# A hybrid convolution and recurrence block on one core: a first stage with joint adaLN scale and shift, and the output gate's steps placed later

## The chip, the cores and the metric

The kernel runs on one core of a Trainium2 chip. The time is the device time of one execution in microseconds (us); where a kernel was run several times, the median counts. A profiled execution gives a trace of every instruction. TensorE is the matrix engine (PE in the rows, PEld is its loading of weights), VectorE is DVE, ScalarE is ACT, GpSimd is POOL, SyncE is SP. ACTq and SPq are DMA issues of these engines.

## The reference, cut to what matters

One layer over 256 latent tokens `x` and 256 context tokens `ctx`, 2048 channels, all float32.

```python
sh, sc, gt = split(silu(c) @ w_ada + b_ada, 3)        # adaLN of the latents; sh_c, sc_c from c_ctx
hn     = rmsnorm(x, norm_g)   * (1 + sc)   + sh
hn_ctx = rmsnorm(ctx, norm_g) * (1 + sc_c) + sh_c
a, g, z_c, xr, z_r, gc, gr = split(hn @ w_in + b_in)  # 2048 columns each
...                                                    # y_conv = conformer(a, g, z_c) @ w_conv_out
...                                                    # y_rnn  = rglru(xr, both directions, state from ctx) * silu(z_r) @ w_rnn_out
y = sigmoid(gc) * y_conv + sigmoid(gr) * y_rnn
x = x + gt * (y @ w_o)
return rmsnorm(x, final_g)
```

For the context only the columns `xr` of `w_in` are needed.

## The kernel before

Channels lie on the 128 partitions in 16 tiles, tokens (256 context, 256 latent) along the free axis. Each float32 operand is split in two parts, `hi` and `lo`, and a product is made of three: hi·hi, hi·lo and lo·hi. For weights ScalarE makes `hi` (`wsplit_hi`, L184) and VectorE `lo` (`wsplit_lo`, L189). For some of them (`adding`, every fourth half from stage AD0 to AD1) `lo` comes instead from ScalarE's negated copy (L195) and a transfer on GpSimd's queue that adds the weight again from DRAM (`wsplit_add`, L196). The order of all work is written out by hand; every engine runs its instructions in the order in which the program emits them, and a transfer waits on the engine that issues it until its buffer is free.

**First stage** (L248 to L370). The input comes in five pieces (L257); the first holds the channel tiles 7 to 4, and the sum of squares `ms` starts with tile 7. VectorE and ScalarE make the squares, TensorE sums them (`stat_mm`, L239), then `1/rms` is made and broadcast (`rms_back`, L290). In parallel the adaLN columns come as 64 pieces `adaraw` of 512 KB, for each group of one or two channel tiles first those of the scale (`part` 1), then those of the shift (`part` 0); TensorE multiplies them by `csil` (`ada_mms`, L220) into one PSUM tile, ScalarE copies it to `row` (L344), and `ada_fin` sums four partial rows with a selector (L227), adds the bias (L229) and forms `(1 + sc) * norm_g` (L232). VectorE scales a tile by `rinv` (L294), applies scale and shift (L300), and `split` gives `xh`, `xl`. The products of a group (`products`, L245: eight output blocks, six of them kept in PSUM banks, two through a spare bank `part` and added by VectorE at L319 and L321) run as a list `todo` while the next group is prepared; TA to TD say how many of them go between which steps.

**Dense part.** 152 stages `s`: the input projection for the recurrence and its gates, for the convolution (`a`, `g`, `z_c`), then five projections with the tokens as output rows in four chunks of 512 columns, four slots of two halves each: `gr`, `rnn`, `gc`, `conv`, `o`. Stage 88 to 103 are `rnn`.

**The output gate.** `gt` for the latents is needed as a row over all partitions, in four chunks of 512 columns. VectorE accumulates it in 64 steps, 16 for a chunk (`gt_step`, L904: `gt_chunk += csil * gt_raw`); a load of 512 KB serves two steps, and two buffers (GTB) hold such loads; the next load is issued when the second step of a pair is emitted. Four calls (GTD) after the last step of a chunk a product with ones (L917) sums the partitions, and ScalarE copies the result back (L918). Steps are called from the slots of the projections: up to GTG in each slot of `gc` (once the side work has started the gate), GTN in each slot of `conv`, GTO in each half slot of `o`. At the chunk's evacuation the rest is forced:

```python
def evac_o(c, i, acc):
    while c not in gt_done:
        gt_steps(1)
```

The last chunk of `o` has two slots of the usual form; its last two slots are written half by half (`for i in range(2)`: 24 products for token half `i`, then `evac_o(3, i, ...)`, then `finish(i)`), without calls of steps besides those of `evac_o`.

Of the kernel before, what the change touches and what calls it, by code (L numbers as in the profile page):

```python
# [8 lines left out]
F32 = mybir.dt.float32  # L9
# [3 lines left out]
PSUM = bass.MemoryType.PSUM  # L13
ADD, MUL, SUB = ALU.add, ALU.mult, ALU.subtract
# [14 lines left out]
GTB, GTG, GTN, GTO, GTD = 2, 2, 2, 1, 4  # L29
TA, TB, TC, TD = 1, 2, 1, 1  # L30
AD0, AD1, ADN = 24, 104, 4
# [53 lines left out]
def block_kernel(ctx, tc, xcat, xtok, fgrow, brow, par, wada, wgt, bgt, wearly, wall, wgate, out):  # L85
# [19 lines left out]
    def pall(name):  # L105
        a, w = _PCOLS[name]
        return pt[:, a:a + w]
# [12 lines left out]
    sh2 = const.tile([P, KT, 2], F32, name="sh2")  # L120
    sc2 = const.tile([P, KT, 2], F32, name="sc2")
# [101 lines left out]
    def ada_fin(row, part, k0, n):  # L223

        tp = ps0.tile([P, 2, 2], F32, tag="ada", name="tp")[:, :n]
        for i in range(n):
            PE.matmul(out=tp[:, i, :], lhsT=row[:, P * i:P * i + P], rhs=pall("sel"), start=True, stop=True)  # L227
        dst = (sh2, sc2)[part][:, k0:k0 + n, :]
        V.tensor_tensor(out=dst, in0=tp, in1=pc("b_ada", 32 * part + 2 * k0, 2 * n).rearrange("p (k v) -> p k v", v=2),  # L229
                        op=ADD)  # L230
        if part == 1:
            V.scalar_tensor_tensor(out=dst, in0=dst, scalar=1.0,  # L232
                                   in1=pc("norm_g", 2 * k0, 2 * n).rearrange("p (k v) -> p k v", v=2),
                                   op0=ADD, op1=MUL)
# [13 lines left out]
    with ExitStack() as st:  # L248
        ps0 = st.enter_context(tc.tile_pool(name="ps0", bufs=1, space=PSUM))
        sp = st.enter_context(tc.tile_pool(name="start", bufs=1))  # L250
        ada_p = st.enter_context(tc.tile_pool(name="ada", bufs=8))
# [4 lines left out]
        for a, b in ((0, 4), (4, 8), (8, 12), (12, 14), (14, 16)):  # L256
            SP.dma_start(out=xlo[:, a:b] if b <= 8 else xhi[:, a - 8:b - 8], in_=xcat[:, a:b, :])  # L257
# [6 lines left out]
        t4 = sp.tile([P, 4], F32, name="t4")  # L264
        A.activation(out=r4[:, 0:1], in_=epst, func=AF.Sqrt)
        ms = psum("ms")
        for n, k in enumerate([*range(7, -1, -1), *range(8, KT)]):
            sq = row_p.tile([P, 512], F32, tag="sq", name="sq", bufs=4)
# [4 lines left out]
            stat_mm(ms, sq, n)  # L273
        sqs = sp.tile([P, 512], F32, name="sqs")
        V.tensor_copy(sqs, ms)
# [5 lines left out]
        rsqrt(r4, t4, s4)  # L281
        dgs = []
        for t in range(4):
            dgs.append(row_p.tile([P, P], F32, tag="dg", name="dg", bufs=4))
            V.tensor_scalar(out=dgs[t], in0=pall("ident"), scalar1=r4[:, t:t + 1], scalar2=None, op0=MUL)

        def rms_back():
            tot = psum("tot")
            for t in range(4):
                PE.matmul(out=tot[:, P * t:P * t + P], lhsT=unit, rhs=dgs[t], start=True, stop=True)  # L290
            return tot

        def scale(k):
            V.tensor_tensor(out=xin(k), in0=xin(k), in1=rinv, op=MUL)  # L294

        def normalise(ks):
            for s in range(2):
                for k in ks:
                    xk = xin(k)[:, T * s:T * s + T]
                    V.tensor_scalar(out=xk, in0=xk, scalar1=sc2[:, k, 1 - s:2 - s], scalar2=sh2[:, k, 1 - s:2 - s],  # L300
                                    op0=MUL, op1=ADD)
            for k in ks:
                split(xh[:, k], xl[:, k], xin(k).rearrange("p (s t) -> p s t", s=2))

        def products(m, ks, ws):
            tr3 = []
            for k, (hi, lo) in zip(ks, ws):
                c = P * m
                tr3 += [(hi[:, c:c + P], xh[:, k]), (hi[:, c:c + P], xl[:, k]), (lo[:, c:c + P], xh[:, k])]
            if m < NPS:  # L310
                mm3(acc0[m].rearrange("p (s t) -> p s t", s=2), ks[0] == 0, ks[-1] == KT - 1, tr3)
# [20 lines left out]
        nraw = 0  # L332
        for j, (k0, n) in enumerate(groups()):
            ks = range(k0, k0 + n)
            ws = []
            for part in (1, 0):
                acc = ps0.tile([P, T], F32, tag="ada", name="ada")[:, :P * n]
                for rnd in range(2 * n):
                    raw = ada_p.tile([P, 1024], F32, tag="ada", name="adaraw")
                    SP.dma_start(out=raw, in_=wada[nraw])  # L340
                    nraw += 1
                    ada_mms(acc, raw, rnd, n)
                row = row_p.tile([P, T], F32, tag="row", name="row", bufs=2)[:, :P * n]
                A.activation(out=row, in_=acc, func=AF.Copy)  # L344
                if part == 1:
                    wr = [load(wearly[k], P * NEARLY) for k in ks]
                    if k0 == 8:
                        parameters()
                run_todo(TA if part else TB)
                if part == 1 and j == 0:  # L350
                    tot = rms_back()
                ada_fin(row, part, k0, n)
                if part == 1 and j == 0:
                    V.tensor_copy(rinv, tot)
                    acc0 = {m: psum(f"xr{m}") for m in range(NPS)}
                    scale(0)
                run_todo(TC if part else TD)
                if part == 1:
                    for k in ks:
                        if k:  # L360
                            scale(k)
                    ws = [wsplit(w, P * NEARLY) for w in wr]
            normalise(ks)
            run_todo(NEARLY)
            if k0 > 8 and prepare:
                prepare.pop(0)()
            todo.extend([lambda m=m, ks=ks, ws=ws: products(m, ks, ws) for m in FIRST])
# [681 lines left out]
    def finish(i):  # L1049
# [118 lines left out]
```

## Time and profile before

| | |
|---|---|
| median of 3 runs | 1126.0 us (1125.2 to 1127.42) |
| profiled execution, its own time | 1123.41 us |
| span of its trace | 1121.6 us |
| TensorE busy | 1094.8 us, 98% |
| VectorE busy | 900.6 us, 80% |
| ScalarE busy | 657.5 us, 59% |
| bytes read | 253.31 MB |

The span is from the first instruction to the last; the own time is 1.8 us more. Rows give a start and a duration in us from the start of the span; durations of matrix records overlap, so a busy TensorE says that it had work, not how dense it was. Behind a row, in brackets, stands how long its engine was idle before it and what ended that. The granted clock column (PEclk) is a share of full speed.

### The profile page before, as it was taken

What the parts mean: (1) busy time and instruction counts of PE and PEld (TensorE: products, weight loads), DVE (VectorE), ACT (ScalarE), POOL (GpSimd) and SP (SyncE); (2) the same over time, 40 slices, a digit from 0 to 9 for tenths busy, and PEclk for the clock granted to TensorE, in tenths of its full rate; (3) what the DMA queues carried; (4) which work ended last, traced back from release to release, by engine and by line L of the source; (5) the groups of instructions that cost most, each with busy time, mean ns of one, the idle gap of its engine ahead of it and who ended that gap; (6) DMA issues with size and microseconds to landing.
All of it is one profiled execution on the core that took longest, in us unless ns stands there. A gap on an engine that the chain in (4) does not pass through costs nothing.

```text
span 1121.6 us, 15861 instructions
## 1 busy us (share of the span) xinstructions
PE 1094.8 (98%) x5788; PEld 876.6 (78%) x5788; DVE 900.6 (80%) x1541; ACT 657.5 (59%) x894; POOL 34.9 (3%) x44
## 2 busy tenths in 40 slices
PE   5999999999999999999999999999999999999996
PEld 3777777777788888788888887888877877788885
DVE  5554587887799787888999899899976967888885
ACT  4222269867788889776565645554536934445443
POOL 0000000000000000000000000000000000000000
PEclk9999999999999999999999999999999999999999
DMA  9998533433355877878888888888874678988872
GB/s 376 398 409 326 220 119 125 132 115 122 106 160 168 209 224 191 230 197 243 238 227 250 219 245 252 227 250 246 238 224 150 191 243 298 322 307 300 287 266 94
DMA packets 74528, 256.45 MB, mean 229 GB/s; under 512 B 8273, under 2 KB 12497, under 8 KB 74065
## 3 DMA queue, kind: packets, MB, share of 16 engines
q1 hardware_dynamic: 68114, 233.42, 61.5%
q0 software_dynamic: 5760, 20.97, 10.4%
q10 hardware_dynamic: 576, 1.05, 0.2%
q8 instruction: 45, 0.74, 0.2%
q14 instruction: 33, 0.27, 0.1%
HBM read 253.31 MB, written 2.10 MB: 228 GB/s over the span
## 4 chain that ended last, share of the span: by engine, by line
PE 79%; DMA 10%; DVE 5%; ACT 2%; issue 2%; SPq 0%; ACTq 0%; DVEq 0%; POOLq 0%
PE acc L602 20%; PE y L613 16%; PE acc L605 10%; PE acc L245 8%; PE o L613 8%; PE xr L245 6%; DMA wlo<-in_wall_dram 5%; PE gate L491 5%; DMA raw<-in_wall_dram 4%; PE ada L220 2%; PE part L245 2%; DVE wlo L189 2%; DVE zc L904 1%; ACT whi L184 1%; PE ms L239 1%
## 5 line engine op out<-in xcount | busy, mean ns | idle before, releaser
L184 ACT ACTIVATE whi<-raw 128x1024 fp32r<-128x1024 f32 x304 | 321.2, 1058 | 300.8 <-PE y L613 79.8
L189 DVE TENSOR_TENSOR wlo<-raw,whi 128x1024 fp32r<-128x1024 f32 x264 | 320.7, 1218 | 64.9 <-ACT whi L184 61.1
L602 PE MATMUL acc<-xx,whi 128*128 128x512 f32 x1024 | 265.0, 401 | 0.0
L613 PE MATMUL y<-whi,xx 128*128 128x512 f32 x1024 | 256.0, 392 | 0.8 <-ACT whi L184 0.8
L613 PEld LDWEIGHTS y<-whi,xx 128*128 128x128 f32 x1024 | 190.8, 188 | 43.5 <-issue 2.5
L602 PEld LDWEIGHTS acc<-xx,whi 128*128 128x128 f32 x1024 | 185.7, 189 | 43.6 <-issue 9.6
L722 DVE SCALAR_TENSOR_TENSOR cv<-hbuf,pt,cv 128x196 f32<-128x196 f32 (+14 forms) x480 | 184.1, 445 | 10.1 <-ACT cv L713 9.7
L605 PEld LDWEIGHTS acc<-xx,wlo 128*128 128x128 f32 x1024 | 139.5, 190 | 11.1 <-DMA wlo<-in_wall_dram 1.1
L605 PE MATMUL acc<-xx,wlo 128*128 128x256 f32 x1024 | 143.0, 282 | 0.3 <-DMA wlo<-in_wall_dram 0.3
L613 PE MATMUL y<-wlo,xx 128*128 128x512 f32 x512 | 137.9, 391 | 3.3 <-DMA wlo<-in_wall_dram 2.7
L613 PEld LDWEIGHTS y<-wlo,xx 128*128 128x128 f32 x512 | 95.5, 188 | 25.8 <-DMA wlo<-in_wall_dram 5.0
L480 DVE SCALAR_TENSOR_TENSOR xc<-xr,pt,xc 128x510 f32<-128x510 f32 (+2 forms) x96 | 70.7, 740 | 0.2
L613 PE MATMUL o<-whi,xx 128*128 128x512 f32 x256 | 65.3, 395 | 0.0
L245 PE MATMUL acc<-xx,whi 128*128 128x512 f32 x256 | 65.2, 407 | 0.0
L245 PE MATMUL xr<-xx,whi 128*128 128x512 f32 x192 | 62.6, 406 | 0.6 <-ACT xx L174 0.4
L491 PE MATMUL gate<-xc,gw 128*128 128x512 f32 x128 | 60.0, 592 | 0.0
L196 POOL DMA_DIRECT2D wlo<-in_wall_dram x40 | 34.6, 866 | 788.8 <-ACT wlo L195 419.2
L245 PEld LDWEIGHTS acc<-xx,whi 128*128 128x128 f32 x256 | 47.8, 188 | 14.2 <-issue 4.8
L613 PEld LDWEIGHTS o<-whi,xx 128*128 128x128 f32 x256 | 47.7, 188 | 10.6 <-issue 0.7
L904 DVE SCALAR_TENSOR_TENSOR zc<-gtraw,csil,zc 128x512 f32<-128x512 f32 x64 | 47.8, 747 | 5.4 <-DMA gtraw<-in_wgt_dram 4.7
L195 ACT ACTIVATE wlo<-raw 128x1024 fp32r<-128x1024 f32 x40 | 41.9, 1049 | 2.5 <-PE y L613 2.0
L344 ACT ACTIVATE row<-ada 128x128 f32<-128x128 f32 (+1 forms) x22 | 7.1, 325 | 60.0 <-PE ada L220 60.0
(178 smaller groups left out, 1048.4 us busy)
## 6 DMA issues: line engine op xcount, KB each, us to landing
raw<-in_wall_dram SPq DMA_DIRECT2D x304, 512.0 KB, 4.5
adaraw<-in_wada_dram SPq DMA_DIRECT2D x64, 512.0 KB, 8.3
wlo<-in_wall_dram POOLq DMA_DIRECT2D x40, 512.0 KB, 7.9
gtraw<-in_wgt_dram SPq DMA_DIRECT2D x32, 512.0 KB, 4.6
raw<-in_wearly_dram SPq DMA_DIRECT2D x16, 512.0 KB, 9.4
gw<-in_wgate_dram SPq DMA_DIRECT2D x32, 128.0 KB, 3.5
hbuf<-in_xcat_dram SPq DMA_DIRECT2D x2, 1024.0 KB, 6.3
gbias<-in_brow_dram SPq DMA_DIRECT2D x8, 256.0 KB, 6.4
```

What stands on the lines that cost most here:

```text
L184: A.activation(out=hi, in_=raw, func=AF.Copy)
L189: V.tensor_tensor(out=lo, in0=raw, in1=hi.bitcast(F32), op=SUB)
L195: A.activation(out=lo, in_=raw, func=AF.Copy, scale=-1.0)
L196: nc.gpsimd.dma_start(out=lo, in_=src, accum_op=ADD)
L245: PE.matmul(out=acc, lhsT=w, rhs=x, start=(first and i == 0), stop=(last and i == n - 1))
L480: V.scalar_tensor_tensor(out=o, in0=i, scalar=w, in1=o, op0=MUL, op1=ADD)
L491: PE.matmul(out=acc, lhsT=u["gw"][:, c:c + 128], rhs=u["xc"], start=True, stop=True)
L602: PE.matmul(out=acc, lhsT=hi[:, 128 * kk:128 * kk + 128], rhs=xx[:, k, 1], start=(k == 0), stop=False)
L605: PE.matmul(out=acc[:, 0], lhsT=lo[:, 128 * kk:128 * kk + 128], rhs=xh[:, k, 1], start=False, stop=(k == KT - 1))
L613: PE.matmul(out=acc, lhsT=y[:, k, seg, P * i:P * i + P], rhs=w[:, 512 * kk:512 * kk + 512], start=(leading and k == 0 and y is xh), stop=( ...
L722: V.scalar_tensor_tensor(out=o, in0=i, scalar=hdw[:, m * CW + j:m * CW + j + 1], in1=o, op0=MUL, op1=ADD)
L904: V.scalar_tensor_tensor(out=gt_chunk(c), in0=gt_raw[0][:, 512 * (k % 2):512 * (k % 2) + 512], scalar=csil[:, k, 0:1], in1=gt_chunk(c), op ...
```

## The change

- Scale and shift of a group are made together: both accumulators in one PSUM tile, one copy to `row`, `PE.transpose` of its tiles and one `tensor_reduce` on VectorE in place of the selector products; the adaLN pieces of both parts come ahead of the group's early weights, ten buffers hold them instead of eight.
- The multiplication by `1/rms` is fused with the scale; the shift is added in the two split operations. `1/rms` is broadcast by a product with a stride-0 operand instead of diagonal tiles.
- The first input piece is issued by ScalarE, the others by SyncE. One adaLN round stands ahead of the end of the sum of squares. The squares take the weights' buffers.
- The list of products is placed anew: TS products ahead of a group's adaLN sums, TA and TB after them, the rest at the end; the first group's list is ordered hi parts first.
- GTN goes from 2 to 1, AD1 from 104 to 98 (37 adding transfers, not 40).
- In `finish` the last of the four output pieces goes from ScalarE to VectorE and SyncE's queue.

```diff
-GTB, GTG, GTN, GTO, GTD = 2, 2, 2, 1, 4
-TA, TB, TC, TD = 1, 2, 1, 1
-AD0, AD1, ADN = 24, 104, 4
+GTB, GTG, GTN, GTO, GTD = 2, 2, 1, 1, 4
+TA, TB = 2, 2
+TS = {1: 5, 2: 2, 3: 1}
+AD0, AD1, ADN = 24, 98, 4
...
+    def ada_fin(row, k0, n):
+
+        tp = ps0.tile([P, 2 * n, P], F32, tag="ada", name="tp")
+        for j in range(2 * n):
+            PE.transpose(tp[:, j], row[:, j // n, P * (j % n):P * (j % n) + P], pall("ident"))
+        red = row_p.tile([P, 2 * n, 2], F32, tag="red", name="red", bufs=2)
+        V.tensor_reduce(out=red, in_=tp.rearrange("p j (q r) -> p j r q", q=4)[:, :, 0:2], axis=AXX, op=ADD)
+        V.tensor_tensor(out=ss2[:, :, k0:k0 + n], in0=red.rearrange("p (a k) v -> p a k v", a=2),
+                        in1=pall("b_ada").rearrange("p (a k v) -> p a k v", a=2, v=2)[:, :, k0:k0 + n], op=ADD)
+        dst = sc2[:, k0:k0 + n]
+        V.scalar_tensor_tensor(out=dst, in0=dst, scalar=1.0,
+                               in1=pc("norm_g", 2 * k0, 2 * n).rearrange("p (k v) -> p k v", v=2), op0=ADD, op1=MUL)
...
-            SP.dma_start(out=xlo[:, a:b] if b <= 8 else xhi[:, a - 8:b - 8], in_=xcat[:, a:b, :])
+            (A if a == 0 else SP).dma_start(out=xlo[:, a:b] if b <= 8 else xhi[:, a - 8:b - 8], in_=xcat[:, a:b, :])
...
+        acc_a = ada_open()
+        ada_sums(acc_a, 1, ada_rounds(1)[:1])
         sqs = sp.tile([P, 512], F32, name="sqs")
-        V.tensor_copy(sqs, ms)
+        V.tensor_copy(sqs[:, :T], ms[:, :T])
+        A.activation(out=sqs[:, T:], in_=ms[:, T:], func=AF.Copy)
...
+        def normalise(ks, rms):
+            xs = [(k, s, xin(k)[:, T * s:T * s + T]) for k in ks for s in range(2)]
+            for k, s, x in xs:
+                V.scalar_tensor_tensor(out=x, in0=x, scalar=sc2[:, k, 1 - s:2 - s], in1=rms[:, T * s:T * s + T],
+                                       op0=MUL, op1=MUL)
+            for k, s, x in xs:
+                A.activation(out=xh[:, k, s], in_=x, func=AF.Identity, bias=sh2[:, k, 1 - s:2 - s])
+            for k, s, x in xs:
+                V.scalar_tensor_tensor(out=xl[:, k, s], in0=x, scalar=sh2[:, k, 1 - s:2 - s],
+                                       in1=xh[:, k, s].bitcast(F32), op0=ADD, op1=SUB)
...
+            run_todo(TS.get(j, 0))
+
+            acc = ada_open() if j else acc_a
+            ada_sums(acc, n, ada_rounds(n)[0 if j else 1:])
+            row = row_p.tile([P, 2, T], F32, tag="row", name="row", bufs=1)[:, :, :P * n]
+            A.activation(out=row, in_=acc[:, :, :P * n], func=AF.Copy)
+            wr = [load(wearly[k], P * NEARLY) for k in ks]
+            if k0 == 8:
+                parameters()
+            run_todo(TA)
+            if j == 0:
+                rms = rms_back()
+            ada_fin(row, k0, n)
+            run_todo(TB)
+            his = [wsplit_hi(w) for w in wr] if j < NS1 else []
+            normalise(ks, rms)
...
+            run_todo(99)
...
-            if c % 2:
+            if c:
                 V.tensor_scalar(out=o, in0=o, scalar1=r, scalar2=None, op0=MUL)
             else:
                 A.activation(out=o, in_=o, func=AF.Copy, scale=r)
-            (SP if c % 2 else A).dma_start(out=out[i, :, 512 * c:512 * c + 512], in_=o)
+            (SP if c else A).dma_start(out=out[i, :, 512 * c:512 * c + 512], in_=o)
```

## Rows read from the trace of the kernel before

**Rows 1.** Timeline of the start: start, duration, engine, line, operation.

```profile
1.18 0.89 SPq L257 DMA_DIRECT2D hbuf<-in_xcat_dram  x2
4.29 0.23 ACT L119 ACTIVATE csil<-pt 128x32 f32<-128x32 f32 x1
6.50 1.15 ACT L272 ACTIVATE sq<-hbuf 128x512 f32<-128x512 f32 x2 [0.48 <-DMA hbuf<-in_xcat_dram]
14.10 0.63 ACT L272 ACTIVATE sq<-xhi 128x512 f32<-128x512 f32 x1 [0.15 <-DMA xhi<-in_xcat_dram]
```

**Rows 2.** Line L239 alone, to 10 us and from 12 to 16 us: ns min/median/max.

```profile
L239 PE MATMUL ms<-sq,ones x10: 1057/1061/1062, 7.3 to 10.0; 128*32 128x512 f32 x10
...
L239 PE MATMUL ms<-sq,ones x16: 592/604/617, 12.2 to 15.3; 128*32 128x512 f32 x16
```

**Rows 3.** Chain that ended last, 14 to 30 us: start, duration, what.

```profile
15.94 0.70 DVE sqs L275
...
18.76 0.18 DVE t L211
...
19.51 1.16 PE tot L290 x8
...
25.93 0.74 PE xr L245 x2
```

**Rows 4.** Busy time by window: engines, PEclk, DMA share, GB/s.

```profile
30.00:40.00 10.00, 10.00 (x101) 7.78 (x100) 6.04 (x14) 2.45 (x5) 0.00 (x0) 1.00 1.03 408
```

**Rows 5.** Chain that ended last, 60 to 180 us.

```profile
60.43 1.86 PE ada L220 x32
62.29 1.58 PE xr L245 x6
63.87 0.34 PE tp L227 x4
...
69.14 1.36 PE xr L245 x6
...
152.00 5.44 PE acc L245 x24
```

**Rows 6.** Timeline near 66.9 us.

```profile
66.91 0.16 PEld L220 LDWEIGHTS ada<-adaraw,csil 128*32 128x32 f32 x8 [0.27 <-DMA adaraw<-in_wada_dram]
```

**Rows 7.** Line L904 by window (gc, conv, o): VectorE busy, count, PEclk, DMA.

```profile
905.00:933.50 28.50, 5.99 (x8) 1.00 0.80 278
933.50:1023.00 89.50, 23.95 (x32) 1.00 0.85 305
1023.00:1122.00 99.00, 17.89 (x24) 0.97 0.64 227
```

**Rows 8.** The gate's loads from 1020 us on.

```profile
DMA to landing us min/median/max: 3.5/4.1/6.0
```

**Rows 9.** Chain that ended last, 1000 to 1122 us.

```profile
1010.20 0.22 PE tps L998 x2
...
1101.62 10.94 PE o L613 x48
...
1117.02 0.72 ACT cv L1063
```

**Rows 10.** Timeline of VectorE in the last projection.

```profile
1073.70 1.22 DVE L189 TENSOR_TENSOR wlo<-raw,whi 128x1024 fp32r<-128x1024 f32 x1
...
1080.90 1.22 DVE L189 TENSOR_TENSOR wlo<-raw,whi 128x1024 fp32r<-128x1024 f32 x1
...
1089.64 0.74 DVE L904 SCALAR_TENSOR_TENSOR zc<-gtraw,csil,zc 128x512 f32<-128x512 f32 x1
...
1096.06 4.62 DVE L189 TENSOR_TENSOR wlo<-raw,whi 128x1024 fp32r<-128x1024 f32 x4
```

**Rows 11.** TensorE's timeline near 832 us, and the window of the conv projection.

```profile
832.76 1.20 PE L613 MATMUL y<-wlo,xx 128*128 128x512 f32 x4 [1.28 <-DMA wlo<-in_wall_dram]
...
926.00:1023.00 97.00, 94.26 (x418) 75.66 (x417) 76.67 (x94) 41.50 (x50) 0.00 (x0) 1.00 0.86 308
```

More of the change, by code (lines that the diff above doesn't have):

```diff
@@ L13 @@
 PSUM = bass.MemoryType.PSUM
+AXX = mybir.AxisListType.X
 ADD, MUL, SUB = ALU.add, ALU.mult, ALU.subtract
@@ L221, in ada_mms @@
                       start=(k < 4), stop=(k >= KT - 4), tile_position=(0, g))
[L223 to L234, printed above, removed]
+    def ada_fin(row, k0, n):
[9 more added lines that the diff above has]
+                               in1=pc("norm_g", 2 * k0, 2 * n).rearrange("p (k v) -> p k v", v=2), op0=ADD, op1=MUL)
     def stat_mm(acc, x, i):
@@ L267, in block_kernel @@
         for n, k in enumerate([*range(7, -1, -1), *range(8, KT)]):
-            sq = row_p.tile([P, 512], F32, tag="sq", name="sq", bufs=4)
+            sq = whl_p.tile([P, 1024], F32, tag="wlo" if k % 2 else "whi", name="sq")[:, :512]
             if k % 2:
@@ L273, in block_kernel, with ada_open, ada_sums, ada_rounds @@
             stat_mm(ms, sq, n)
+        nraw = [0]
+        def ada_open():
+            return ps0.tile([P, 2, T], F32, tag="ada", name="ada")
+        def ada_sums(acc, n, rounds):
+            for part, rnd in rounds:
+                raw = ada_p.tile([P, 1024], F32, tag="ada", name="adaraw")
+                SP.dma_start(out=raw, in_=wada[nraw[0]])
+                nraw[0] += 1
+                ada_mms(acc[:, part], raw, rnd, n)
+        def ada_rounds(n):
+            return [(part, rnd) for part in (1, 0) for rnd in range(2 * n)]
+        acc_a = ada_open()
+        ada_sums(acc_a, 1, ada_rounds(1)[:1])
         sqs = sp.tile([P, 512], F32, name="sqs")
-        V.tensor_copy(sqs, ms)
+        V.tensor_copy(sqs[:, :T], ms[:, :T])
+        A.activation(out=sqs[:, T:], in_=ms[:, T:], func=AF.Copy)
         s4 = psum("s4")[:, :4]
@@ L280, in block_kernel @@
             PE.matmul(out=s4[:, t:t + 1], lhsT=sqs[:, P * t:P * t + P], rhs=sel4[:, :1], start=True, stop=True)
[L281 to L285, printed above, removed]
+        A.activation(out=r4, in_=s4, func=AF.Sqrt, bias=epst)
+        V.tensor_scalar(out=v4, in0=s4, scalar1=EPS, scalar2=-0.5, op0=ADD, op1=MUL)
+        V.reciprocal(out=r4, in_=r4)
+        V.tensor_tensor(out=t4, in0=r4, in1=r4, op=MUL)
+        V.tensor_tensor(out=t4, in0=t4, in1=v4, op=MUL)
+        V.scalar_tensor_tensor(out=r4, in0=t4, scalar=1.5, in1=r4, op0=ADD, op1=MUL)
         def rms_back():
@@ L289, in rms_back, with products @@
             for t in range(4):
-                PE.matmul(out=tot[:, P * t:P * t + P], lhsT=unit, rhs=dgs[t], start=True, stop=True)
-            return tot
[L293 to L305, printed above, removed]
+                r = r4[:, t:t + 1]
+                PE.matmul(out=tot[:, P * t:P * t + P], lhsT=bass.AP(r.tensor, r.offset, [r.ap[0], [0, P]]), rhs=pall("ident"),
+                          start=True, stop=True)
+            return tot
+        def normalise(ks, rms):
[8 more added lines that the diff above has]
+                                       in1=xh[:, k, s].bitcast(F32), op0=ADD, op1=SUB)
+        def products(m, ks, ws, which=(0, 1, 2)):
             tr3 = []
@@ L308, in products @@
                 c = P * m
-                tr3 += [(hi[:, c:c + P], xh[:, k]), (hi[:, c:c + P], xl[:, k]), (lo[:, c:c + P], xh[:, k])]
+                tr3 += [((hi, hi, lo)[w][:, c:c + P], (xh, xl, xh)[w][:, k]) for w in which]
             if m < NPS:
-                mm3(acc0[m].rearrange("p (s t) -> p s t", s=2), ks[0] == 0, ks[-1] == KT - 1, tr3)
+                mm3(acc0[m].rearrange("p (s t) -> p s t", s=2), ks[0] == 0 and 0 in which, ks[-1] == KT - 1, tr3)
                 return
@@ L330, in run_todo @@
                 todo.popleft()()
-        nraw = 0
         for j, (k0, n) in enumerate(groups()):
             ks = range(k0, k0 + n)
[L335 to L364, printed above, removed]
@@ L365, in block_kernel @@
+            ada_fin(row, k0, n)
+            run_todo(TB)
+            his = [wsplit_hi(w) for w in wr] if j < NS1 else []
+            normalise(ks, rms)
+            if j == 0:
+                A.activation(out=rinv, in_=rms, func=AF.Copy)
+                rms = rinv
+                acc0 = {m: psum(f"xr{m}") for m in range(NPS)}
+            ws = [(hi, wsplit_lo(w, hi)) for w, hi in zip(wr, his)] if his else [wsplit(w, P * NEARLY) for w in wr]
+            run_todo(99)
             if k0 > 8 and prepare:
@@ L366, in block_kernel @@
                 prepare.pop(0)()
-            todo.extend([lambda m=m, ks=ks, ws=ws: products(m, ks, ws) for m in FIRST])
+            if j:
+                todo.extend([lambda m=m, ks=ks, ws=ws: products(m, ks, ws) for m in FIRST])
+            else:
+                for which in ((0, 1), (2,)):
+                    todo.extend([lambda m=m, ks=ks, ws=ws, which=which: products(m, ks, ws, which) for m in range(NPS)])
+                todo.extend([lambda m=m, ks=ks, ws=ws: products(m, ks, ws) for m in range(NPS, NEARLY)])
```

7 lines of the change are left out of this document (4 added, 3 removed).

## The prediction, as it was made

> **What bounds the kernel now.** I read the page first (shares by engine, the slices), then the chain of waits for three stretches, then the timeline of single engines. TensorE is busy for 98% of the span and the chain is TensorE from 25.93 us to the last projection's end; so only three places can move the time: the start, where TensorE waits for its first dense product; a few stalls in the dense part; and the tail after 1112.56 us. In the start the reader is to see that the squares are summed as the input lands, the last piece at 14.1 us, and that the dense products begin at 25.93 [rows 1, 3]. From there the first stage runs on TensorE without gaps until 152.0 [rows 5], but the transfers run at 408 GB/s with the engines full [rows 4], and once TensorE waited for an adaLN piece, at 66.91 [rows 6]. So the first stage is bound twice, by products and by bytes. Last, the output gate: of its 64 steps 8 run in the gc projection, 32 in the conv projection, 24 in the last one [rows 7]; 24 is 8 per chunk in three chunks, one per half slot.
>
> **First stage: its start.** The first megabyte of the input is now issued by ScalarE, whose program has the SiLU of c ahead of it, which ends at 4.52 [rows 1]; SyncE issued it at 1.18. The sums start with just this piece. Before, it took 5.3 us from issue to landing (1.18 to 6.5) [rows 1]. Bounds: alone on the engines it lands at 4.55 + 5.3 = 9.9; behind everything else of the input at 14.1. The two are far apart and no row has two such queues at once; I take the middle, 12.0. A square takes some 0.7. The 16 matmuls of the sum are 32 records; the first ten after the idle start took 1061 ns, the later ones 604 [rows 2], so the clock was at the lower of its levels in the first of them. At 1.36/6 = 0.23 us a record [rows 5] and double for ten, 32 x 0.22 + 10 x 0.22 = 9.2 us: the sum ends at 21.9, against 15.92.
> From there the joint path is shorter. Before: copy to first broadcast product 15.94 to 19.51, 3.6 us, and on to 25.93 [rows 3]. Now the copy is split and covered by an adaLN round, one small operation of 0.18 goes [rows 3], the diagonal tiles go: 3.1. Then broadcast 1.16 [rows 3], two transposes 0.25, three small operations 0.6, half a scaling 0.4, two ScalarE halves 0.8: 6.3 in all, dense at 28.2 instead of 25.93, with one adaLN block more still to do (half of a pair's 1.86 [rows 5], so 1.0).
> The Trainium skill (DMA: Bandwidth & Descriptors, section Issuing engines are not separate DMA queues) speaks against an early transfer by another engine: all issuing engines feed the same 16 DMA engines, and a second one saves only issue time. By its round robin between queues in the section Queues, rings and completion order the piece would land near 11.8, an estimate, and the sum would stay as it is; no run here shows two such queues side by side.
>
> **First stage: its products.** From 25.93 to 152.0 are 126.1 us. After each adaLN block the next six records take 1.58 instead of 1.36, 0.22 lost [rows 5]; 19 blocks become 10, so -2.0. The small products with the selector (0.34 for a pair of channel tiles [rows 5], a third of it for one) were 4.5 in all and some 0.1 of hand-over after each of the 19; 30 transposes at 0.11 [rows 9] and ten hand-overs make 4.3: -2.1. One more block +1.0. One new wait: the first group's list is reordered, so that its two products that go through the single spare PSUM bank stand next to each other; the second waits for VectorE to empty it (0.70 [rows 3]) behind the weight's low part (1.22 [rows 10]) and that group's scaling, some 2.2 by estimate, bounds 0.7 and 3. Sum 126.1 - 2.0 - 2.1 + 1.0 + 2.2 = 125.2; 28.2 + 125.2 = 153.4, say +1.0 against 152.0 with the small waits that go. VectorE's scaling pass, which folds into the next operation, was under TensorE's products and is priced at nothing; without that cover it would be 16 x 0.7.
> Bytes set the lower bound. Two early weights (1.05 MB) now stand behind the adaLN piece that TensorE waited for; at 408 GB/s it lands 2.6 us sooner, at 64.3. After it as much work is left as before, plus the two products that used to run between the two blocks, less the savings of later groups: the stage can't end before 149.5. So the term is **+1.0, bounds -2.5 and +4**. Ten adaLN buffers for eight change nothing there, since the engines are full.
>
> **Adding transfers.** The three left out are the last ones of the rnn projection. One of them stalled TensorE for 1.28 us [rows 11]. Its replacement is 3 x 1.22 us of VectorE, which waits there for TensorE and ScalarE, and 3 copies of ScalarE less. **-1.3, bounds -1.8 and 0.**
>
> **Conv projection with half the steps.** 16 steps of 0.75 us and eight 512 KB loads leave it. SyncE's load of a gate piece waits for the step that frees its buffer, and the weights behind it wait too. TensorE was idle for 97.0 - 94.3 = 2.7 us from 926 to 1023 [rows 11]; all of it could go. **-2.7, bounds -3.6 (some slips hide in modelled ends) and 0.**
>
> **Last projection.** 40 steps are left for it, not 24, and the rate is still one per half slot: 8 in each of three chunks and 4 in the two slots of the fourth, 28. The other 12 are forced by the loop in evac_o that calls a step until the chunk's gate is there. Four stand ahead of the third chunk's evacuation, since the sum for it is held back by four calls; eight stand ahead of the fourth's, at the very end, where nothing is left to hide them; and the gate's product stands in TensorE's queue ahead of the second half's last 24 products. In times of before, along VectorE: the 24th step ends at 1090.3 [rows 10]. Of the four forced, two have data; the other pair's load could only be issued at 1090.4, when its buffer came free, and lands 3.6 us later (fastest 3.5, median 4.1, [rows 8]): 1094.0, plus two steps 1.5: 1095.5. The evacuation of two halves takes 1090.3 to 1096.06 [rows 10], 5.75: 1101.25. Four pairs of split and step at 1.8 (1073.70 to 1080.90 are four [rows 10]) and one more split: 1109.6. Eight steps, whose loads are two buffers deep, 3.6 us from step to landing: two at once (1111.1), the next load lands at 1112.0 (1113.5), then 1114.7 (1116.2), then 1117.1: the last step ends at 1118.6. The gate product 0.9 and 24 products 10.94/2 [rows 9]: 1125.0, against 1112.56. What follows took 9.0 us to the span's end at 1121.6: +12.4. TensorE has been idle for some 8 us then; ten records at the lower clock cost 10 x 0.22 = 2.2 as in the start [rows 2]. Moving the last scaling from ScalarE (1117.02 [rows 9]) to VectorE gives back 0.5. **+14.1; bounds: no load waited for, 1119.7 + 9.0, +6.6; median landings and all 26 products at half clock, +21.4.**
>
> **Sum.** +1.0 - 1.3 - 2.7 + 14.1 = +11.1. The profiled execution was 1123.4 and would be 1134.5; it is 2.6 below the median of the runs, and what is compared is medians: 1126.0 + 11.0 = **1137.0 us**.
>
> **Rivals.**
> (a) The forced steps' loads are hidden, and only VectorE's time counts: +1.0 - 1.3 - 2.7 + 6.6 = +3.6, 1129.6. For it: the transfers take only 0.64 of the engines there [rows 7]. Against: two buffers, each freed only by the step before. 0.14.
> (b) The first stage reaches its bound of bytes (the first piece lands early, no bank wait): 1137.0 - 3.5 = 1133.5. Against: ScalarE's place in the queue. 0.13.
> (c) The clock stays low for the whole last half and landings are slower: 1126 - 3.0 + 21.4 = 1144.4. 0.10.
> (d) The other side: VectorE runs the gate's steps ahead in the time when it waits for TensorE, so that the last gate is there when the first half is summed. Then the tail costs nothing and 1126 - 2.5 - 1.8 - 3.6 = 1118. It decides where the 64th step ends before 1107; the sum turns at a tail under 3.0 us. Against: a call per half slot is written out, and each step needs its load. 0.08.
> The forecast has 0.55.
>
> **How the numbers follow.** A measurement of this kernel tells 0.2%, 2.3 us, from no change. Faster is (d), 0.08; within it, the low end of (a), 0.04; slower the rest, 0.88. The range leaves out (d), (c) beyond its low end and the edge of (a): 1129 to 1143.
>
> **What would show it.** Gate steps: 8, 16 and 40 by projection; a group of eight in the last 20 us with VectorE idle between pairs for the gate's load; TensorE waiting at the gate's product for some 8 us, and slow records after it. In the start, the first square at about 12 instead of 6.5, ScalarE's issue at 4.5, dense products at 28. No stall at the end of the rnn projection; fewer in conv. It is wrong if the gate's last step ends well before 1107 in times of before, or if the first stage ends more than 3 us sooner than 152.

## The result, and the profile of the kernel after

The changed kernel takes 1136.5 us in the median of four runs (1135.26 to 1138.45); four runs of the kernel before, beside it, gave 1125.6. The ratio is 1.0115, with a 95% interval from 1.0093 to 1.0137: 1% slower. The forecast was 1137.0, between 1129 and 1143. The profiled execution took 1135.26 us, its span 1133.5; TensorE was busy for 1089.1 us of it (96%), VectorE for 897.8 (79%), ScalarE for 657.9 (58%).

The timeline of the kernel after, at the start, at the new waits of TensorE in the first stage and the dense part, and in the tail; it answers to [rows 1, 10]:

```profile
3.02 1.28 ACT L121 ACT_TABLE_LOAD   x1 [3.02 <-DMA pt<-in_par_dram]
3.08 0.39 ACTq L260 DMA_DIRECT2D hbuf<-in_xcat_dram  x1
...
11.98 2.19 ACT L276 ACTIVATE sq<-hbuf 128x512 f32<-128x512 f32 x4 [5.93 <-DMA hbuf<-in_xcat_dram]
...
12.72 6.37 PE L242 MATMUL ms<-sq,ones 128*32 128x512 f32 x32 [12.72 <-DVE sq L274]
...
35.87 0.72 PE L248 MATMUL part<-xx,whi 128*128 128x512 f32 x2 [2.60 <-DVE hbuf L344]
...
530.80 1.22 PE L626 MATMUL acc<-xx,wlo 128*128 128x256 f32 x8 [1.93 <-DMA wlo<-in_wall_dram]
...
1090.46 1.54 DVE L925 SCALAR_TENSOR_TENSOR zc<-gtraw,csil,zc 128x512 f32<-128x512 f32 x2 [3.10 <-DMA gtraw<-in_wgt_dram]
...
1115.69 2.08 PE L938 MATMUL gps<-zc,unit 128*128 128x512 f32 x2 [8.50 <-DVE zc L925]
1116.78 2.69 PE L634 MATMUL o<-whi,xx 128*128 128x512 f32 x4
```

The records of the sum up to 16 us answer to [rows 2]:

```profile
L242 PE MATMUL ms<-sq,ones x16: 1060/1061/1062, 12.7 to 15.9; 128*32 128x512 f32 x16
```

ScalarE issues the first piece at 3.08, while its table load runs, not after the SiLU. It lands at 11.95, and all squares start behind it. The 32 records of the sum then run in 6.4 us, 0.20 each, though the first sixteen are 1.06 us long.

The chain that ended last, for the start, the borders of the stages and the tail; it answers to [rows 3, 5, 9]:

```profile
3.08 8.87 DMA hbuf<-in_xcat_dram
...
12.72 6.42 PE ms L242 x32
...
20.70 1.45 PE ada L223 x48
22.15 1.09 PE tot L315 x8
...
25.57 0.51 PE xr L248
...
151.37 3.64 PE acc L248 x16
...
155.03 1.07 ACT whi L187
156.10 0.71 ACT xc L489
156.81 0.35 issue
157.15 1.96 PE gate L512 x4
...
655.69 1.15 PE y L634 x5
...
1018.80 2.72 PE o L634 x12
...
1104.97 3.46 DMA gtraw<-in_wgt_dram
...
1110.08 3.55 DMA gtraw<-in_wgt_dram
...
1114.10 0.76 DVE zc L925
...
1115.69 2.08 PE gps L938 x2
1117.77 6.65 PE o L634 x24
...
1124.44 0.70 DVE hbuf L1061
```

Dense products start at 25.57 (before, the chain has them from 25.93; by the timeline a single one ran there at 25.20 already), the first stage ends at 151.37 (before 152.0), and then a wait for the gate's input takes most of this back. At the end the reader is to see a chain that was not there before: a load of a gate weight, two steps, a load, two steps, the gate's product, and then 24 products that nothing covers.

The gate's steps by window (the steps that the slots of gc, conv and o call; VectorE busy, count, PEclk, DMA share, GB/s) answer to [rows 7]:

```profile
905.00:933.50 28.50, 5.99 (x8) 1.00 0.77 267
933.50:1020.00 86.50, 11.91 (x16) 1.00 0.82 295
1020.00:1133.00 113.00, 29.79 (x40) 0.91 0.63 221
```

The gate's loads in the last projection, and VectorE's idle time ahead of the steps (us, times), answer to [rows 8]:

```profile
  DMA gtraw<-in_wgt_dram: 6.6, 4
...
DMA to landing us min/median/max: 3.3/3.7/5.4
```

The steps are 8, 16 and 40. The forced group ahead of the third evacuation waits 3.1 us for a load; the one at the end leaves TensorE idle for 8.5 us, and the four products behind the gate's take 2.69 us; the 24 of this half take 6.65, where a half of the 48 of before took 5.47 [rows 9].

By stages, from the two chains: start and first stage up to the first dense product after the gates (168.01 against 168.09) -0.1; dense part up to `gr` (655.69 against 653.83) +1.9; `gr` and `rnn` -0.3; `gc` and `conv` -5.2 (by the first product of each, -0.4 and -4.8); the last projection, from its first to its last product 105.6 us against 90.1, +15.5; what follows 9.06 against 9.02. The sum is +11.9, the difference of the spans.

### The profile page after: what moved, and what is told of

It is laid out like the page before. It is cut to its first block, busy times and chain, and to the rows that moved or that the text cites. A ratio compares the mean times of both kernels' runs of the same rounds, so it can differ in the third digit from the quotient of the medians.

```text
span 1133.5 us, 15754 instructions
## 1 busy us (share of the span) xinstructions
PE 1089.1 (96%) x5756; PEld 877.1 (77%) x5756; DVE 897.8 (79%) x1541; ACT 657.9 (58%) x896; POOL 32.3 (3%) x41
## 4 chain that ended last, share of the span: by engine, by line
PE 83%; DMA 8%; DVE 4%; ACT 2%; issue 2%; SPq 0%; DVEq 0%; ACTq 0%
PE y L634 27%; PE acc L623 18%; PE acc L626 10%; PE acc L248 8%; PE xr L248 5%; PE gate L512 5%; PE o L634 5%; DMA wlo<-in_wall_dram 4%; PE ada L223 2%; PE part L248 2%; DMA raw<-in_wall_dram 1%; DVE zc L925 1%; DMA gtraw<-in_wgt_dram 1%; DVE wlo L192 1%; DMA adaraw<-in_wada_dram 1%
## 5 line engine op out<-in xcount | busy, mean ns | idle before, releaser
L187 ACT ACTIVATE whi<-raw 128x1024 fp32r<-128x1024 f32 x308 | 325.3, 1058 | 296.7 <-PE y L634 101.5
L192 DVE TENSOR_TENSOR wlo<-raw,whi 128x1024 fp32r<-128x1024 f32 x271 | 329.4, 1218 | 59.0 <-ACT whi L187 58.5
L634 PE MATMUL o<-whi,xx 128*128 128x512 f32 x256 | 68.0, 406 | 0.0
L248 PE MATMUL xr<-xx,whi 128*128 128x512 f32 x192 | 60.3, 398 | 2.1 <-ACT xx L325 2.1
L199 POOL DMA_DIRECT2D wlo<-in_wall_dram x37 | 32.1, 867 | 761.8 <-ACT wlo L198 392.4
L248 PEld LDWEIGHTS xr<-xx,whi 128*128 128x128 f32 x192 | 35.1, 188 | 12.3 <-issue 2.9
L198 ACT ACTIVATE wlo<-raw 128x1024 fp32r<-128x1024 f32 x37 | 38.8, 1048 | 5.2 <-PE y L634 3.2
## 6 DMA issues: line engine op xcount, KB each, us to landing
raw<-in_wearly_dram SPq DMA_DIRECT2D x16, 512.0 KB, 10.2
```

Source lines behind the costliest of these rows:

```text
L187: A.activation(out=hi, in_=raw, func=AF.Copy)
L192: V.tensor_tensor(out=lo, in0=raw, in1=hi.bitcast(F32), op=SUB)
L198: A.activation(out=lo, in_=raw, func=AF.Copy, scale=-1.0)
L199: nc.gpsimd.dma_start(out=lo, in_=src, accum_op=ADD)
L248: PE.matmul(out=acc, lhsT=w, rhs=x, start=(first and i == 0), stop=(last and i == n - 1))
L634: PE.matmul(out=acc, lhsT=y[:, k, seg, P * i:P * i + P], rhs=w[:, 512 * kk:512 * kk + 512], start=(leading and k == 0 and y is xh), stop=( ...
```

## The experiments

The table gives the last projection's length by TensorE's timeline (first to last product), VectorE's waits for gate loads in it, and the ratio to the kernel before, run beside it. In the kernel before the projection takes 90.3 us and has no such wait.

| run | steps conv / o | o, us | gate waits, us | median, us | ratio [95%] |
|---|---|---|---|---|---|
| after | 16 / 40 | 105.8 | 6.6 | 1136.5 | 1.0115 [1.0093, 1.0137] |
| e1 | 16 / 40 | 107.2 | 7.3 | 1136.3 | 1.0120 [1.0098, 1.0142] |
| e2 | 32 / 24 | 90.3 | 0 | 1124.6 | 1.0017 [0.9998, 1.0036] |
| e3 | 16 / 40, even | 105.1 | 10.2 | 1137.0 | 1.0126 [1.0094, 1.0158] |
| e4 | 16 / 40, last 8 loads out | 100.1 | 0 | 1130.7 | 1.0068 [1.0043, 1.0093] |
| e5 | 16 / 40, even, adding | 105.0 | 21.6 | 1137.4 | 1.0116 [1.0085, 1.0147] |
| e6 | 24 / 32, even | 96.9 | 7.5 | 1126.2 | 1.0030 [1.0016, 1.0044] |
| e7 | 16 / 40 | 105.7 | 5.9 | 1133.6 | 1.0091 [1.0070, 1.0111] |
| e8 | 32 / 24 | 90.3 | 0 | 1122.3 | 0.9991 [0.9972, 1.0009] |
| e9 | 16 / 40, even, o's loads out | 92.3 | 0 | 1123.7 | 1.0000 [0.9975, 1.0024] |
| e10 | 32 / 24 | 90.3 | 0 | 1120.9 | 0.9980 [0.9958, 1.0001] |
| e11 | 16 / 40 | 94.0, product after it | 6.7 | 1136.3 | 1.0104 [1.0068, 1.0140] |
| e12 | 16 / 40, even, other queue | 107.8 | 14.9 | 1135.3 | 1.0102 [1.0069, 1.0135] |

**The gate's steps alone, and the rest alone.** The kernel before with

```diff
-GTB, GTG, GTN, GTO, GTD = 2, 2, 2, 1, 4
+GTB, GTG, GTN, GTO, GTD = 2, 2, 1, 1, 4
```

> The kernel before with GTN 1 alone: 16 gate steps in the conv projection and 40 in the last one, first stage and adding transfers as before. Theory A (the twelve steps that evac_o forces at the end set the loss): the conv projection ends some 5 us earlier, the last projection takes some 15 us longer, so about +10, 1135 to 1137 us, and the trace shows TensorE waiting some 8 us for the gate's product. Theory B (the new first stage or the three missing adding transfers cost the time): this kernel is within 3 us of the one before, 1123 to 1128 us.

and the changed kernel with the same line turned back:

> The changed kernel with GTN back at 2: only the new first stage, the 37 adding transfers and the new finish are left. By the differences of the two traces at the ends of the stages (start and first stage -0.1, dense middle +1.9, gr and rnn -0.3, finish 0) theory A gives +1.5, about 1127 us, and no wait at the gate's product. The prediction's own terms (+1.0, -1.3, -0.5) give -0.8, 1124.8 us. Theory B gives some +10, 1135 us.

e1 has the whole loss (1.0120), e2 none of it (1.0017). Theory B falls: the move of the steps is the loss, and the new first stage, the 37 transfers and the new finish together are within what can be told from no change. Whether it is the forced steps, as theory A has it, these two runs do not tell. TensorE waited 8.4 us at the gate's product in e1, and for nothing in e2's last projection. In e1:

```profile
1116.39 2.08 PE L917 MATMUL gps<-zc,unit 128*128 128x512 f32 x2 [8.37 <-DVE zc L904]
```

**Placed evenly.** The changed kernel with 12, 14 and 14 steps called in the first three chunks (those of the fourth are not needed then):

```diff
-                gt_steps(GTO)
+                gt_steps(GTO + (h == 0 if c == 0 else (kq, h) in ((0, 0), (0, 1), (1, 0), (2, 0), (2, 1), (3, 0)) if c < 3 else 0))
```

> The changed kernel with the 40 steps of the last projection called evenly, 12, 14 and 14 in its first three chunks, so that none is forced at an evacuation; loads, buffers and step count are unchanged. Theory A1 (it is the place of the twelve forced steps, with each load waited for): the tail of 15 us goes almost wholly, 1121 to 1124 us, since the gain in the conv projection stays. Theory A2 (VectorE has no room for more than 8 steps in a chunk: splits 9.1, evacuation 5.75, 8 steps 6.0 of 21.8 us, so six more steps a chunk are 4.5 us over and TensorE waits for low parts of weights instead): most of the loss comes back in the middle of the projection, 1128 to 1134 us, with TensorE's waits now on wlo.

The idle time at the end was gone, and the time was the same. TensorE's and VectorE's longest waits of e3 in the last projection (us in total, times, longest):

```profile
PE o L634 <- DVE wlo L192: 8.5, 3, 4.4
...
DVE zc L925 <- DMA gtraw<-in_wgt_dram: 10.2, 9, 1.9
```

TensorE now waited in the middle, for low parts of weights that stood behind VectorE's waits. A1 fell: the place of the forced steps is not the cause. A2 had the waits for `wlo` right, but the time is above its range (1137.0 against 1128 to 1134), and the second row already speaks for the loads beside VectorE's work. TensorE's waits are 8.5 of the 14.8 us by which the projection is longer; behind the last of them its records also ran at the lower clock (granted 0.50 from 1110 to 1115 us).

**Loads left out, forced order.** In `gt_load` of the changed kernel:

```diff
+        if n >= 24:
+            gt_raw.append(gt_raw[-1])
+            return
```

> The changed kernel with the last eight loads of gate weights left out (the steps from the 49th on read the 24th load's data again, so the gate's last chunk is wrong by that); the steps, their order and their places stay. Theory A1 (the loads, two buffers deep, set half of the loss): VectorE's 6.6 us of waits at the steps go (3.1, 1.0, 1.1 and 1.4), and the kernel takes 1129 to 1131 us, TensorE waiting some 3 to 5 us at the gate's product. Theory A2 (VectorE's own work sets it): under 2 us come back, 1134 to 1136.5 us.

5.6 us of the last projection came back (105.8 to 100.1), TensorE waited 5.4 us at the gate's product instead of 8.5, and the median is in A1's range. So the loads' waits are worth about what VectorE's rows show of them (6.6 us); the forced steps themselves, TensorE's clock behind them (granted 0.50 from 1110 to 1115 us) and the late evacuation are the rest.

**VectorE relieved.** e3 with adding transfers in the last projection too, seven of them:

```diff
-        return AD0 <= s < AD1 and (2 * s + h) % ADN == ADN - 1
+        return (AD0 <= s < AD1 or 136 <= s < 151) and (2 * s + h) % ADN == ADN - 1
```

> The even placing of the 40 steps (12, 14 and 14) and, in the last projection too, adding transfers for every fourth half of a weight: seven or eight splits of 1.22 us, 8.5 to 9.8 us in all, leave VectorE, and transfers on GpSimd's queue make these low parts. Theory A2 (VectorE's time in the last projection sets the loss): those 8.5 us come back and some 4 us more of waits that queue behind, so 1121 to 1128 us. Theory A3 (the loads of gate weights, 10.2 us of VectorE's waits in the even placing, set it): VectorE only waits longer for them, 1131 to 1136 us.

Nothing came back, as A3 had it (1137.4 us, a little above its range). VectorE had 8.5 us less to do and waited for gate loads 21.6 us instead of 10.2; these loads took 5.3 us from issue to landing in the median and 9.7 at most, where e3's took 4.4 and 6.3, and TensorE waited 6.4 us for the new transfers themselves.

**Fewer steps moved.** 24 steps in conv (2 and 1 by turns), 10, 11 and 11 in the last projection:

```diff
-        gt_steps(GTN)
+        gt_steps(1 + (kq % 2 == 0))
...
-                gt_steps(GTO)
+                gt_steps(GTO + ((kq, h) in ((0, 0), (2, 0), (3, 0))[:2 + (c > 0)] if c < 3 else 0))
```

> The changed kernel with 24 steps in the conv projection (2 and 1 by turns) and 32 in the last one (10, 11 and 11 in its chunks, none forced). Theory A2 (VectorE is full with 8 steps a chunk, a step beyond costs its 0.75 us and a share of a load's wait): eight steps beyond cost 6 to 8 us less what slack there was, and the conv projection keeps 2 to 4 of its 5 us; 1122 to 1128 us. Theory A4 (there is no limit by work, only the forced group at the end costs): all of the conv gain stays and nothing is lost, 1118 to 1121 us.

1126.2 us, inside A2's range: the last projection was 6.7 us longer than before, 0.83 a step, with 7.5 us of waits for loads (in a profiled execution of 1130.6 us, the longest of the twelve). A4 fell.

**No loads in the last projection.** e3 with the lines of e4 at `n >= 14`:

> The even placing (12, 14 and 14 steps) with all loads of gate weights left out that fall in the last projection (from the 15th on the steps read the 14th load's data again, so the gate's later half is wrong by that). Theory A2 (VectorE's own work sets the 15 us of the even placing): 16 steps more at 0.75 us are 12 us, so it stays at 1128 to 1134 us, TensorE waiting for wlo. Theory A3 (the loads set it: two buffers, each freed only by a step, behind the weights in SyncE's queue): the 10.2 us of VectorE's waits go and TensorE hardly waits, 1118 to 1125 us.

The loss went: 1123.7 us, ratio 1.0000, and the last projection took 92.3 us. TensorE's only wait in it, on its timeline:

```profile
1096.59 1.19 PE L634 MATMUL o<-wlo,xx 128*128 128x512 f32 x4 [0.91 <-DVE wlo L192]
```

VectorE does the 16 more steps nearly for free, 2.1 us, as long as their data are there. A2 fell, A3 holds: the loads are the loss.

**Another queue.** Is it SyncE's queue that makes them late? e3 with the first input piece on SyncE (e7) and

```diff
-        SP.dma_start(out=raw, in_=wgt[n])
+        nc.gpsimd.dma_start(out=raw, in_=wgt[n])
```

> The even placing (12, 14 and 14 steps, none forced), first input piece on SyncE, and all loads of gate weights issued by GpSimd, whose queue then holds nothing else; number and size of loads and buffers unchanged. Theory Q (the loads come late because they stand in SyncE's queue behind weight loads that wait 43.6 us for VectorE's splits, and the weights behind them): the waits of 10.2 us go or fall under 3, TensorE hardly waits in the last projection, 1117 to 1122 us. Theory B2 (two buffers, each refilled only 3.5 us or more after its second step, whatever the queue): the waits stay at 8 to 12 us and the kernel at 1130 to 1135 us.

Theory Q fell: nothing came back. B2 has the cause, but not the size: the waits were longer than its 8 to 12 us, and the time is just above its range (1135.3 against 1130 to 1135). VectorE's wait for loads, GpSimd's and SyncE's for buffers, in e12's last projection:

```profile
DVE zc L925 <- DMA gtraw<-in_wgt_dram: 14.9, 11, 2.6
...
POOL gtraw L913 <- DVE zc L925: 70.9, 17, 10.7
...
SPq L182 <- DVE wlo L192: 84.5, 25, 7.2
```

Each load on its own queue stands waiting for VectorE's step that frees its buffer, and VectorE then waits for the load. On SyncE's queue it was no different: in e3 every gate load of the last projection was issued within 0.1 us of the end of the step that freed its buffer, so the queue did not hold it.

What counts is the turn-around. With two buffers the load of a pair starts when the second step of the pair two ahead of it is done, and must land before VectorE, with one pair between, comes to it. In the kernel before, VectorE came to a pair 4.6 us or more after that start, mostly over 6, the loads took 3.5 to 6.0 [rows 8], and it never waited. In e3 it came to 14 of the 20 pairs after 3.6 to 4.8 us, and the loads took:

```profile
DMA to landing us min/median/max: 3.5/4.4/6.3
```

In e6 the shortest of these times are 3.7 us, and VectorE waited in seven places. A third buffer was not tried. Leaving the loads out in e9 also takes their bytes off the engines; but a load's median landing is 4.4 us in e3 against 4.1 before, while the time left for it shrank by more, which speaks for the turn-around.

**The gate's product behind the last products.** The changed kernel with

```diff
-        evac_o(3, i, accs[i])
-        finish(i)
+    for i in range(2):
+        evac_o(3, i, accs[i])
+        finish(i)
```

> The changed kernel with the second half's last 24 products placed ahead of the last chunk's gate product in TensorE's queue, both evacuations behind it; the twelve forced steps stay. If the loss is VectorE's late end of the steps (the last at 1115.6 us), only what followed it on TensorE goes: 1118.4 for the copied gate, two evacuations of 2.2 us, then the finish of one half, some 1129.5 for the span's end against 1133.5, so 4 us less than the changed kernel, 1131 to 1133.5 us, and no slow records. If the idle TensorE and its clock were all of it, 1126 us.

From the last projection's first product to the span's end it took 113.7 us, against 114.9: 1.2 came back, not 4, and in the median no difference that can be told (1136.3 us, above the expected range). The estimate let the second evacuation follow the first at once; in VectorE's queue the first half's `finish` stands between. The chain of e11:

```profile
1115.80 2.09 PE gps L938 x2
1117.91 0.61 ACT zc L939
1118.54 0.70 DVE hbuf L1061
...
1123.11 0.61 DVE hbuf L1061
```

Taking TensorE's wait ahead of the last 24 products out of the end thus wins little here: 4.6 us of VectorE, the first half's evacuation and `finish`, take its place on the chain.

**The early transfer.** The changed kernel with the first input piece on SyncE:

```diff
-            (A if a == 0 else SP).dma_start(...)
+            SP.dma_start(...)
```

> The changed kernel with the first piece of the input issued by SyncE again, as the other four. Theory S1 (the piece's place on ScalarE's queue delays the squares from 6.5 to 12 us and is the cost of the new start): the sum ends some 3 to 4 us earlier, the dense products start at 22 to 23 us, and the first stage ends 2 to 3 us before 151.4; the kernel gains at most as much, since TensorE waits at the first gates after the stage. Theory S2 (the sum of squares ends with the last piece of the input and the bytes set the stage's end): dense products start some 2 us earlier, the stage ends within 1 us of 151.4, the kernel takes the time of the changed one within 1 us.

The first squares started at 6.14 instead of 11.98, the dense products at 22.88 instead of 25.57:

```profile
6.14 1.15 ACT L276 ACTIVATE sq<-hbuf 128x512 f32<-128x512 f32 x2 [0.23 <-DMA hbuf<-in_xcat_dram]
```

The stage ended at 151.1, 0.2 earlier: in this trace S2. TensorE waited three times, 1.7 us in all, for adaLN pieces, and its clock was low from 33 to 36 us (granted 0.50). But the stage's end varies: e12 has the same first stage, kept the full clock in it, waited 0.9 us for pieces and ended it at 148.6, as S1 had it. The ratio is 0.24% lower than the changed kernel's, some 2.7 us where S2 allows 1, with intervals that overlap.

Why does the piece land so late from ScalarE's queue? In the changed kernel, packets, MB and share of the DMA engines' time of SyncE's queue (q1) and ScalarE's (q10), first from 3 to 6.5 us, then from 6.7 to 11.3:

```profile
q1 hardware_dynamic: 181, 1.35, 93.0%
...
q10 hardware_dynamic: 139, 1.04, 53.5%
q1 hardware_dynamic: 166, 0.87, 45.4%
```

Issued at 3.08, nothing of the piece moved before 6.5 us, while SyncE's pieces kept the engines; then both queues moved at about the same rate. To see what is left of the whole, e7's line and GTN 2 were put together:

> The changed kernel with GTN 2 and the first piece of the input issued by SyncE, that is the new first stage without its early transfer on ScalarE's queue, 37 adding transfers, the new finish, and the gate's steps as before. By the two runs that changed one of these each (the ratios to the kernel before were 1.0017 with GTN 2, and 1.0091 for SyncE's piece against 1.0115) it stands at 0.9993, 1122 to 1125 us, no change that can be told. If the joint scale and shift save TensorE what the prediction counted (-2.0 and -2.1 us) and the bytes do not hold the stage, 1119 to 1121 us.

1120.9 us, ratio 0.9980. It is the fastest version of the study, but the interval reaches 1.0001. The median lies in the second range of the expectation, yet its condition is not shown: in the profiled execution the dense products started at 24.09 and the stage ended at 153.2, with a low clock on the way (last section). Three pairs differ by this one line (e7 and after, e10 and e2, e12 and e3 but for the queue): 0.24, 0.37 and 0.24% less with SyncE's piece. The two intervals of each pair overlap; that all three point one way speaks for the early transfer on ScalarE's queue costing rather than bringing.

**The adding transfers alone.** The kernel before with AD1 98:

> The kernel before with 37 adding transfers, nothing else changed. By the prediction's term TensorE's wait of 1.28 us at 832.8 us goes and the kernel gains 1.3 us. The rival, by the changed kernel's trace (gr and rnn together 0.3 us shorter, the waits at the transfers kept there longer): within 0.5 us of the kernel before, since the wait moves to another transfer.

0.9991, no difference that can be told. The wait at 832.8 us is not in its trace; TensorE's waits for `wlo` from `gr` to `conv` are 1.0 us in two times, where before had 2.7 in four. By the first products the `rnn` projection took 88.5 us in e8 and in the changed kernel, 90.5 before, but 89.0 in e1, which has all 40 transfers. So neither -1.3 nor nothing is excluded by the times, and the traces put the gain of that projection at 0.5 to 2.0.

## Why the prediction came out right, and where its terms were off

**The last projection, +14.1 and measured +15.5.** This is the step that decided, and it ran as written: 8, 16 and 40 steps; four forced ahead of the third evacuation with a load waited for (3.1 us); eight at the end, two with data and then load by load; the gate's product; 24 products at the low clock first (granted 0.50 from 1115 to 1120 us). The forecast had the last step 96.2 us after the projection's start (1118.6 on 1022.4), the trace has 96.8 (1115.6 on 1018.8). The gate's product and 24 products were to take 0.9 + 5.5 + 2.2 = 8.6 and took 8.7. Of the difference of 1.4 us, 0.5 is the finish, which gained nothing (9.06 us against 9.02), since its last operation only changed engine on a chain of the same length.

**What was not seen in it.** The prediction took the forced place for the cause. e3 shows that the same 40 steps cost as much when none is forced, and e9 that the loads do it. The condition of rival (d), that the 64th step ends before 1107 in times of before, was met in e3 by calling the steps earlier: there it ended at 1102.3. No step was forced at the end then, but the price was paid by TensorE's waits for weights instead. Rival (a), hidden loads, is e4: +9.9 in the last projection where (a) had +6.6; (a) had left out the low clock, which e4 pays as well.

**Conv, -2.7 and measured -4.8.** The stage's idle time before was 2.7 us in its window [rows 11] and the stage got 4.8 shorter: products were also spaced wider without a gap that the timeline shows as idle. From execution to execution it varies; by first products `conv` took 93.5 to 95.7 us in the four traces with 32 steps (before, e2, e8, e10) and 90.7 to 92.1 in the nine with 16. The means, 94.7 and 90.9, differ by 3.8. So the gain is real, and the prediction had it too small.

**Adding transfers, -1.3 and measured -0.3.** `rnn` got 2.0 us shorter and `gr`, which still has its transfers and waits longer for them, 1.7 us longer.

**Start, +2.3 predicted and -0.4 measured.** This is against the 25.93 that the prediction took for the first dense product; from first product to first product it is +0.4 (25.57 against 25.20). The landing at 12.0 was right (11.95) by two errors that cancel: ScalarE issued at 3.08 and not at 4.55, and the transfer took 8.87 us and not 7.4. By the Trainium skill (DMA: Bandwidth & Descriptors, section Queues, rings and completion order) the DMA engines take turns between the queues, and the piece would land near 11.8, an estimate made for an issue at 4.55. The trace agrees with the turns, 1.04 MB beside 0.87 while the piece moved, but not with the 7.3 us that the estimate leaves for the transfer: the piece first stood still for over 3 us. Why it did stayed open. The step that failed is the sum of squares, "32 x 0.22 + 10 x 0.22 = 9.2 us": records of 1.06 us overlap and came every 0.20 us, so the sum took 6.4.

**Products of the first stage, 125.2 and measured 125.8.** The wait at the spare bank was 2.6 (predicted 2.2). The stage's end in the profiled execution is 2.0 earlier than forecast, from the start. Over the eight traces with this first stage and its early transfer the stage ends at 152.7 in the mean by the timeline, over the three with the old one at 152.0: +0.7, near the predicted +1.0, but with a clock that fell in some of them (below). The bound of bytes was set too late: in e12, with a start 2.7 us sooner, the stage ended at 148.6, ahead of the 149.5 that the prediction held for the earliest end, though TensorE waited for pieces there too.

**Not foreseen: +1.9 in the dense middle.** An adding transfer at 530.80 came 1.93 us late; e2 has the same wait, 1.7. Which shift of the first stage made it late stayed open.

That the total came within half a us of the median is in part luck: the terms were off by -1.1, +1.9, +1.0, -2.5 (`gc` and `conv`) and +1.4, which leaves +0.7.

## What to carry to other kernels

Before moving streamed steps into a stage, compare the refill time of a buffer (issue to landing, from the trace) with the time that the stage leaves between two uses of it; with two buffers a step rate beyond that made the consuming engine wait here, in both placements and on both queues that were tried. An engine with enough idle time by its busy share can still be unable to take more work when that work brings a load. And when a stage has no slack, test a suspected cost by leaving the load out, not by moving the step.

## What the runs showed of the hardware that was not expected

- In five of the eleven traces with the new first stage the granted clock was 0.74 to 0.83 between 25 and 45 us (e3, e5, e6, e10, e11; in e7 0.91, in the other five 1.00). The stretch in e3, in the changed kernel and in the kernel before (PE, PEld, DVE, ACT and POOL busy, PEclk, DMA share, GB/s):

```profile
25.00:45.00 20.00, 16.95 (x171) 12.69 (x172) 7.71 (x16) 4.43 (x8) 0.00 (x0) 0.83 0.96 372
```

```profile
25.00:45.00 20.00, 16.81 (x182) 12.80 (x182) 10.16 (x22) 5.48 (x11) 0.00 (x0) 1.00 1.03 407
```

```profile
25.00:45.00 20.00, 19.58 (x220) 14.84 (x224) 11.93 (x25) 5.53 (x11) 0.00 (x0) 1.00 1.03 408
```

  A mean of 0.83 is the lower of the two levels (1.2 instead of 2.4 GHz) for a third of the stretch. TensorE had waited 2.1 us ahead of its first dense product and 2.6 at the spare bank in all eleven. In e3 these waits ended at 25.43 and 37.26, and the low stretches begin within some 1 us of these ends:

```profile
26.50:29.80 3.30, 3.30 (x12) 2.09 (x14) 0.53 (x1) 0.00 (x0) 0.00 (x0) 0.50 1.01 402
...
36.80:40.00 3.20, 2.74 (x7) 2.16 (x8) 1.10 (x2) 0.00 (x0) 0.00 (x0) 0.50 1.03 410
```

  With the old start TensorE was busy for 19.4 to 19.8 of the 20 us, and none of the three traces shows the low clock. The stage ended at 153.2 to 155.5 in the five traces and at 148.6 to 151.8 in the others. That the two waits bring the fall is argued from its place; no run takes them out, and the same waits left the clock high in five traces. Of the eight traces with the early transfer the four with the low clock end the stage 2.2 us later than the old start, the four without it 0.8 sooner: this is what the mean of +0.7 is made of.
- The first matrix records of the sum of squares are 1.06 us long, but 32 of them ran in 6.4 us, one every 0.20 us: they overlap, and a record's length is no measure of the pace. The prediction took such a length for the lower clock; the granted clock column shows 1.00 from 12.7 to 17 us, so no row shows it there.
- An engine's transfer stands in its queue and not behind its table load: ScalarE issued at 3.08, 0.06 us after the parameters had landed, while its table load ran from 3.02 to 4.30.
- By the Trainium skill (DMA: Bandwidth & Descriptors, section Issuing engines are not separate DMA queues) a second issuing engine saves only the time of the issue. Both tries agree: e12's loads took 4.9 us from issue to landing on GpSimd's queue against 4.4 on SyncE's, and the input piece on ScalarE's took 8.87 against 4.93 in e7.
